# Three results of VectorE stay in PSUM banks: GLA's cumulative decay, the head norm's reciprocal root, and the SSD group's masked C.B

## The chip, the cores and the metric

The kernel runs on one core of one Trainium2 chip. Five engines of that core share the work, each with its own instruction stream: TensorE (PE in the profile, its weight loads PEld), VectorE (DVE), ScalarE (ACT), GpSimd (POOL) and SyncE (SP), which issues the transfers. There are two on-chip memories: SBUF, where operands live, and PSUM, eight banks of 128 x 512 fp32, where TensorE leaves its sums. The metric is the device time of one launch in microseconds.

## The reference

A decoder trunk of two layers over 1024 tokens, model width 1024, inner width 2048, all in float32. Layer 0 mixes tokens by gated linear attention (GLA), layer 1 by a Mamba-2 SSD mixer. Cut to what matters:

```
h = rmsnorm(x); q, k, v, g, low = split(h @ w_in)
a = log_sigmoid(low @ w_gate_up + bias) / 16          # 4 heads of 128 keys
# GLA, per chunk and head; S is the state (128 keys x 512 values)
b = cumsum(a)                                          # cumulative decay
attn = sum_d q[i,d] * k[j,d] * exp(b[i,d] - b[j,d])    # j <= i
o = (q * exp(b)) @ S + attn @ v
S = exp(b_last) * S + (k * exp(b_last - b)).T @ v
x = x + (rmsnorm(o) * head_norm * silu(g)) @ w_out     # head norm: mean over 512 values

# SSD, per group (8 groups of 4 heads), a = cumsum(dt * A)
y = (C B^T * exp(a_i - a_j), j <= i) @ (x * dt) + exp(a) * (C @ H) + x * d_skip
H = exp(a_last) * H + B.T @ (x * dt * exp(a_last - a))
x = x + rmsnorm(y * silu(z)) @ w_out
out = rmsnorm(x)
```

## The kernel before

Everything is held feature-major: a tile is 128 features by 512 tokens, so 1024 tokens are two passes t = 0 and t = 1, in the order GLA(0), GLA(1), SSD(0), SSD(1).

**Weight work.** The large projections run in three products per tile, from operands split into a high and a low part: high x high, low x high, high x low (`mm3`, L223 to L225, and L469 to L471 for v). A *unit* is one weight block of 128 x 512: its raw block is loaded (`wraw`), ScalarE makes the high half (`wh`, L171), and in the first pass GpSimd makes the low half (`wl`, L176) and SyncE stores it to DRAM; in the second pass the low half is loaded from there, and GpSimd has none of that work. `run` goes through the units one by one. The PSUM banks of the weight work have the tag "pp" (four), those of the mixers "mb" (four). Whatever empties a bank (`evac`) comes one unit later: in GLA L419 for the gate, L444 for q, L478, L480 and L482 for v (L478 on ScalarE in the first pass; in the second L480 on VectorE and L482 on ScalarE by turns), and L515, which adds an output projection to the residual.

**Sides.** The token mixers are generators that `run` steps at a given rate between units (0.95 steps a unit for a GLA head, 1.1 for an SSD group). So a mixer's instructions stand between the weight work of the next head or group. This is only the program's order: the framework's scheduler, which simulates a time line, then sets the final order of every engine's stream from the dependences and from when it expects operands. A tag with n buffers gives an n-th later tile the same memory, so it has to wait for the last reader of the earlier one.

**GLA's mixer, one head (L525 to L746).** L540 multiplies the low-rank gate into bank z. ScalarE and VectorE make log-sigmoid from it, and L551 scans it into b, an SBUF tile (`m2`). From b come, each as a subtraction on VectorE, an exponential on ScalarE and a multiplication on VectorE:

- kd (L558 to L560), the keys for the state, transposed by TensorE at L626;
- qd (L563, L564), the queries for the state;
- d (L569 to L573), keys and queries half a chunk apart;
- keys and queries at distances s = 16, 4 and 1 (L579 to L581 and L597 to L601; the queries of s = 16 and 4 are the tiles `o`, those of s = 1 the two tiles `raw`).

The products (L655) multiply keys by queries into four mb banks at once, VectorE places the results by masks (L616, L620) and from there attention, state (L712) and output o follow. Then the head norm: squares are summed on GpSimd (L321), `rstd_steps` spreads the sum over partitions with two matmuls into an mb bank p (L292, L293), `rstd_of` and `newton` (L307 to L313) make the reciprocal root. Its result r is an SBUF tile `rstd`. L738 multiplies o by the norm's weight and r, L739 (GpSimd) by the gate, and L743 and L744 split the product y into its two parts for the output projection.

**The SSD mixer, one group.** L1005 multiplies B and C into bank `pcb`. L1017 masks that to the lower triangle, into the SBUF tile `cbm` (`m2`). Four decay matrices M, one per head (two at L1044, two at L1067), are multiplied by it on VectorE and go into TensorE as operands. L1053 and L1055 advance the state H, L1028 and L1035 make the inputs.

What decides the order around the change is thus the scheduler, and the number of banks: four mb banks that z, the transposes, the products, the norm's p and the SSD's `pcb` take by turns.

Of the kernel before, what the change touches and what calls it, by code (L numbers as in the profile page):

```python
# [13 lines left out]
AF = mybir.ActivationFunctionType  # L14
ALU = mybir.AluOpType

P = 128
# [36 lines left out]
def hybrid_kernel(ctx: ExitStack, tc: tile.TileContext, xT, w_in0, w_gk, w_up, w_out0,  # L54
# [28 lines left out]
    def c3(ap, w=P):  # L83
        return ap.rearrange("p (n w) -> p n w", w=w)
# [198 lines left out]

    def rstd_steps(ssum, n, box, var=None):

        hi, lo = tl("t", NTMP, dt=F32R)[:], tl("t", NTMP, dt=F32R)[:]
        A.copy(hi, ssum)
        V.tensor_tensor(lo, ssum, hi.bitcast(F32), op=ALU.subtract)  # L290
        p = ps("mb")
        PE.matmul(p[:], onr[:], hi, start=True, stop=False)  # L292
        PE.matmul(p[:], onr[:], lo, start=False, stop=True)  # L293
        yield
        yield from rstd_of(p, n, box, var)

    def rstd_of(p, n, box, var):
        v = tmp() if var is None else var
        V.tensor_scalar(v, p[:], 1.0 / n, EPS, op0=ALU.mult, op1=ALU.add)
        r = tl("rstd", 3)[:]  # L300
        l = tmp()
        act(l, v, AF.Ln)
        act(l, l, AF.Exp, scale=-0.5)
        newton(V, r, v, l)
        box.append(r)
        yield
# [102 lines left out]
    class Gla:  # L409
# [115 lines left out]
        def mixer(self, h):  # L525
# [23 lines left out]
            for c in range(NC):  # L549
                cs = slice(c * P, (c + 1) * P)  # L550
                V.tensor_tensor_scan(b[:, cs], m[:, cs], l[:, cs], 0.0, op0=ALU.add, op1=ALU.subtract)  # L551
            yield

# [3 lines left out]
            kd = tmp()  # L557
            V.tensor_tensor(c3(kd), bc[:, :, P - 1:P].to_broadcast([P, NC, P]), bc, op=ALU.subtract)  # L558
            act(kd, kd, AF.Exp, scale=1.0 / 16)
            V.tensor_tensor(kd, k, kd, op=ALU.mult)  # L560
            yield
            qd = tl("x", 4)[:]
            act(qd, b, AF.Exp, scale=1.0 / 16)  # L563
            V.tensor_tensor(qd, q, qd, op=ALU.mult)  # L564
# [3 lines left out]
            dv = c3(d)  # L568
            V.tensor_tensor(dv, bc, bc[:, :, 63:64].to_broadcast([P, NC, P]), op=ALU.subtract)  # L569
            act(dv[:, :, 0:64], dv[:, :, 0:64], AF.Exp, scale=-1.0 / 16)  # L570
# [4 lines left out]
            def keys(s):  # L575

                e = tmp()
                bv = c3(b, s)
                V.tensor_tensor(c3(e, s), bv[:, :, s - 1:s].to_broadcast([P, T // s, s]), bv, op=ALU.subtract)  # L579
                act(e, e, AF.Exp, scale=1.0 / 16)  # L580
                V.tensor_tensor(e, k, e, op=ALU.mult)  # L581
                return e

            def queries(s, e, c0=0, c1=NC):
# [5 lines left out]
                cs = slice(c0 * P, c1 * P)  # L590
                bv, qv = c3(b[:, cs], w), c3(q[:, cs], w)
                after = []
                for i in range(3):
                    f, l = (i + 1) * s, 4 * s
                    o = sum(4 * s - (m + 1) * s for m in range(i))
                    after.append((e[:, :, o:o + l - f], f))
                    V.tensor_tensor(after[-1][0], bv[:, :, f:l], bv[:, :, f - 1:f].to_broadcast([P, n, l - f]),  # L597
                                    op=ALU.subtract)
# [131 lines left out]
            box = []  # L730
            yield from rstd_steps(ss, 512, box)
            for g in self.g[h]:
# [16 lines left out]
    class Ssd:  # L749
# [151 lines left out]
        def mixer(self, g):  # L901
# [110 lines left out]
            for c in range(NC):  # L1012
                for i in range(2):
                    o = (c % 2) * 256 + i * P
                    PE.transpose(px[c // 2][:, o:o + P], X[i][:, c * P:(c + 1) * P], ident[:])
            cbm = tl("m2", 1)[:]
            V.tensor_tensor(c3(cbm), c3(pcb[:]), trim[:].unsqueeze(1).to_broadcast([P, NC, P]), op=ALU.mult)  # L1017
            bh, bl = tl("ktok", 1, dt=F32R)[:], tl("t", NTMP, dt=F32R)[:]
# [383 lines left out]
```

## Time and profile before

| | |
|---|---|
| three runs | 1627.66, 1629.36, 1630.39 us; median 1629.36 |
| profiled execution | 1634.13 us, span 1632.4 us, mean granted clock of TensorE 0.992 |
| span by stage (from the trace) | first 69 us: norm, q, k and v of the first head; 69 to 421: GLA heads of t = 0; 421 to 770: GLA heads of t = 1; then SSD |

In the page's lines of groups a row reads: line, engine, operation, output <- inputs by the program's names, shape and type of both, how many; then, behind the bar, busy time in us and the mean ns of one; behind the second bar the idle time of the engine just before, and what ended most of it. In the lists of waits a row says which engine waited, at which tile and line, for which engine, tile and line, and then the us in all, the number of waits, and the longest one. A timeline row begins with the start in us from the span's start and the duration in us of that many instructions (x4). A row of a table by windows has the window's bounds, its length, the busy us and number of instructions of PE, PEld, DVE, ACT and POOL, the granted clock, the busy share of the DMA engines and what they moved in GB/s.

### The profile page before, as it was taken

What the parts mean: (1) busy time and instruction counts of PE and PEld (TensorE: products, weight loads), DVE (VectorE), ACT (ScalarE), POOL (GpSimd) and SP (SyncE); (2) the same over time, 40 slices, a digit from 0 to 9 for tenths busy, and PEclk for the clock granted to TensorE, in tenths of its full rate; (3) what the DMA queues carried; (4) which work ended last, traced back from release to release, by engine and by line L of the source; (5) the groups of instructions that cost most, each with busy time, mean ns of one, the idle gap of its engine ahead of it and who ended that gap; (6) DMA issues with size and microseconds to landing.
All of it is one profiled execution on the core that took longest, in us unless ns stands there. A gap on an engine that the chain in (4) does not pass through costs nothing.

```text
span 1632.4 us, 23995 instructions
## 1 busy us (share of the span) xinstructions
PE 1580.0 (97%) x8272; PEld 1308.2 (80%) x8272; DVE 984.5 (60%) x1579; ACT 947.2 (58%) x1788; POOL 692.8 (42%) x542
## 2 busy tenths in 40 slices
PE   7998999999999999999999999999999999999996
PEld 5777887877887888878888888887878888888886
DVE  6457567495736436295855534467885973355657
ACT  4435364543726355464874766665757777667843
POOL 6457566563412121126545655665523232222322
PEclk9999999999999999999999999999999999999999
DMA  7634556364585556463587555566666776656762
GB/s 232 185 123 131 176 174 201 123 201 146 191 269 193 162 166 217 154 207 120 176 262 228 175 188 173 173 209 216 208 193 186 257 235 221 204 177 189 260 197 84
DMA packets 172746, 309.30 MB, mean 189 GB/s; under 512 B 19088, under 2 KB 25104, under 8 KB 172624
## 3 DMA queue, kind: packets, MB, share of 16 engines
q1 hardware_dynamic: 172624, 307.77, 59.2%
q8 instruction: 65, 1.06, 0.3%
q14 instruction: 57, 0.47, 0.1%
HBM read 232.06 MB, written 75.63 MB: 188 GB/s over the span
## 4 chain that ended last, share of the span: by engine, by line
PE 78%; DVE 11%; ACT 4%; DMA 3%; issue 2%; POOL 2%; SPq 0%; DVEq 0%; ACTq 0%; POOLq 0%
PE pp L223 19%; PE pp L225 19%; PE pp L224 19%; PE pp L469 3%; PE pp L470 3%; PE pp L471 3%; PE mb L953 2%; PE mb L706 2%; DMA wraw<-w_in 2%; PE mb L705 2%; PE mb L946 1%; PE mb L655 1%; POOL wl L176 1%; PE mb L224 1%; PE mb L223 1%
## 5 line engine op out<-in xcount | busy, mean ns | idle before, releaser
L171 ACT CAST wh<-wraw 128x512 fp32r<-128x512 f32 x472 | 289.3, 618 | 379.3 <-PE pp L224 154.2
L223 PE MATMUL pp<-hh,wh 128*128 128x512 f32 x1184 | 468.3, 396 | 13.2 <-ACT wh L171 7.5
L176 POOL TENSOR_TENSOR wl<-wraw,wh 128x512 fp32r<-128x512 f32 x240 | 352.6, 1478 | 268.6 <-ACT wh L171 233.7
L224 PE MATMUL pp<-hl,wh 128*128 128x512 f32 x1184 | 464.1, 392 | 1.6 <-DVE hl L371 1.3
L225 PE MATMUL pp<-hh,wl 128*128 128x512 f32 x1184 | 463.2, 392 | 0.0
L223 PEld LDWEIGHTS pp<-hh,wh 128*128 128x128 f32 x1184 | 222.8, 188 | 65.3 <-ACT wh L171 9.0
L224 PEld LDWEIGHTS pp<-hl,wh 128*128 128x128 f32 x1184 | 222.9, 188 | 49.2 <-DVE hl L371 3.2
L225 PEld LDWEIGHTS pp<-hh,wl 128*128 128x128 f32 x1184 | 222.8, 188 | 46.5 <-issue 0.3
L223 PE MATMUL pp<-yh,wh 128*128 128x512 f32 x448 | 180.5, 403 | 5.2 <-DVE sg L419 2.4
L225 PE MATMUL pp<-yh,wl 128*128 128x512 f32 x448 | 178.5, 399 | 4.6 <-POOL wl L176 4.6
L224 PE MATMUL pp<-yl,wh 128*128 128x512 f32 x448 | 177.3, 396 | 0.0
L321 POOL TENSOR_TENSOR ss<-ss,t 128x512 f32<-128x512 f32 x53 | 74.4, 1403 | 81.7 <-ACT t L320 70.4
L223 PEld LDWEIGHTS pp<-yh,wh 128*128 128x128 f32 x448 | 85.6, 191 | 26.2 <-issue 4.5
L225 PEld LDWEIGHTS pp<-yh,wl 128*128 128x128 f32 x448 | 85.6, 191 | 24.4 <-POOL wl L176 5.1
L469 PE MATMUL pp<-wh,hh 128*128 128x512 f32 x256 | 100.8, 395 | 2.7 <-DVE m L444 2.7
L470 PE MATMUL pp<-wl,hh 128*128 128x512 f32 x256 | 101.0, 394 | 0.0
L471 PE MATMUL pp<-wh,hl 128*128 128x512 f32 x256 | 100.3, 394 | 0.0
L224 PEld LDWEIGHTS pp<-yl,wh 128*128 128x128 f32 x448 | 85.4, 191 | 18.2
L824 DVE SCALAR_TENSOR_TENSOR m<-pp,pr,m 128x509 f32<-128x509 f32 (+2 forms) x96 | 70.3, 742 | 40.0 <-ACT m L821 38.9
L824 DVE SCALAR_TENSOR_TENSOR x<-pp,pr,x 128x509 f32<-128x509 f32 (+2 forms) x96 | 71.2, 743 | 33.3 <-ACT x L821 32.2
L645 POOL TENSOR_TENSOR t<-v,t 128x512 fp32r<-128x512 f32 x28 | 40.6, 1460 | 101.5 <-ACT t L644 65.7
L739 POOL TENSOR_TENSOR t<-t,sg 128x512 f32<-128x512 f32 x32 | 50.9, 1621 | 75.3 <-ACT sg L98 68.3
(284 smaller groups left out, 2654.0 us busy)
## 6 DMA issues: line engine op xcount, KB each, us to landing
wraw<-w_in SPq DMA_DIRECT2D x352, 256.0 KB, 3.5
low_in<-wl SPq DMA_DIRECT2D x176, 256.0 KB, 3.8
wl<-low_in SPq DMA_DIRECT2D x176, 256.0 KB, 3.4
wraw<-w_out SPq DMA_DIRECT2D x128, 256.0 KB, 3.6
low_out<-wl SPq DMA_DIRECT2D x64, 256.0 KB, 4.3
v<-a_cum SPq DMA_DIRECT2D x64, 256.0 KB, 3.8
wl<-low_out SPq DMA_DIRECT2D x56, 256.0 KB, 3.4
xn<-x SPq DMA_DIRECT2D x43, 256.0 KB, 3.8
```

What stands on the lines that cost most here:

```text
L171: A.copy(hi[:, 0:w], raws[n][:, 0:w])
L176: G.tensor_tensor(lo[:, 0:w], raws[n][:, 0:w], hi[:, 0:w].bitcast(F32), op=ALU.subtract)
L223: PE.matmul(o, lh, rh, start=first, stop=False)
L224: PE.matmul(o, lh, rl, start=False, stop=False)
L225: PE.matmul(o, ll, rh, start=False, stop=last)
L321: eng.tensor_tensor(ss, ss, sq, op=ALU.add)
L469: PE.matmul(o, rh[kb][:, cs], wh[:], start=(kb == 0), stop=False)
L470: PE.matmul(o, rh[kb][:, cs], wl[:], start=False, stop=False)
L471: PE.matmul(o, rl[kb][:, cs], wh[:], start=False, stop=(kb == KB - 1))
L645: G.tensor_tensor(vl, v[c], vh.bitcast(F32), op=ALU.subtract)
L739: G.tensor_tensor(u, u, self.g[h][vb], op=ALU.mult)
L824: V.scalar_tensor_tensor(dst[:, s:], o[:, 0:T - s], col(C_CW + j * 32 + si), dst[:, s:], op0=ALU.mult, op1=ALU.add)
```

## The change

Three results are written to, or left in, a PSUM bank, so that the VectorE instructions that read them take one operand from PSUM and one from SBUF instead of two from SBUF.

1. **b.** After the scan ScalarE copies b into bank z, which until then held the gate's product (`A.copy(z[:], b)`, L553). Every subtraction (kd, d, keys, queries) takes its full-size operand from z, and its broadcast column still from b in SBUF; the exponential for qd reads z. The bank is held until the last of them.
2. **The head norm.** With `stay=True` the last instruction of `newton` writes r over p, the bank of the norm's sums. The four multiplications by r (L738, now L741) read it there. The other norms keep their SBUF tile.
3. **Masked C.B.** L1017 masks `pcb` in place; the four multiplications read it there. The tile `m2` isn't taken in SSD for it any more.

```diff
-        yield from rstd_of(p, n, box, var)
+        yield from rstd_of(p, n, box, var, stay)
 ...
-    def rstd_of(p, n, box, var):
+    def rstd_of(p, n, box, var, stay=False):
         v = tmp() if var is None else var
         V.tensor_scalar(v, p[:], 1.0 / n, EPS, op0=ALU.mult, op1=ALU.add)
-        r = tl("rstd", 3)[:]
+        r = p[:] if stay else tl("rstd", 3)[:]
 ...
                 V.tensor_tensor_scan(b[:, cs], m[:, cs], l[:, cs], 0.0, op0=ALU.add, op1=ALU.subtract)
+
+            A.copy(z[:], b)
+            bz, zc = z[:], c3(z[:])
             yield
 ...
-            V.tensor_tensor(c3(kd), bc[:, :, P - 1:P].to_broadcast([P, NC, P]), bc, op=ALU.subtract)
+            V.tensor_tensor(c3(kd), bc[:, :, P - 1:P].to_broadcast([P, NC, P]), zc, op=ALU.subtract)
 ...
-            act(qd, b, AF.Exp, scale=1.0 / 16)
+            act(qd, bz, AF.Exp, scale=1.0 / 16)
 ...
-            V.tensor_tensor(dv, bc, bc[:, :, 63:64].to_broadcast([P, NC, P]), op=ALU.subtract)
+            V.tensor_tensor(dv, zc, bc[:, :, 63:64].to_broadcast([P, NC, P]), op=ALU.subtract)
 ...
-                V.tensor_tensor(c3(e, s), bv[:, :, s - 1:s].to_broadcast([P, T // s, s]), bv, op=ALU.subtract)
+                V.tensor_tensor(c3(e, s), bv[:, :, s - 1:s].to_broadcast([P, T // s, s]), c3(bz, s), op=ALU.subtract)
 ...
-                    V.tensor_tensor(after[-1][0], bv[:, :, f:l], bv[:, :, f - 1:f].to_broadcast([P, n, l - f]),
+                    V.tensor_tensor(after[-1][0], zv[:, :, f:l], bv[:, :, f - 1:f].to_broadcast([P, n, l - f]),
                                     op=ALU.subtract)
 ...
-            yield from rstd_steps(ss, 512, box)
+            yield from rstd_steps(ss, 512, box, stay=True)
 ...
-            cbm = tl("m2", 1)[:]
-            V.tensor_tensor(c3(cbm), c3(pcb[:]), trim[:].unsqueeze(1).to_broadcast([P, NC, P]), op=ALU.mult)
+            cbm = pcb[:]
+            V.tensor_tensor(c3(cbm), c3(cbm), trim[:].unsqueeze(1).to_broadcast([P, NC, P]), op=ALU.mult)
```

Lines behind L551 are three higher in the changed kernel: L558 is now L561, L560 is L563, L597 is L600, L601 is L604, L626 is L629, L655 is L658, L738 is L741. The scheduler orders GLA's mixers anew; in SSD it leaves almost everything in place. Three places, all in the first head of t = 0 (b is the tile m_134, z is mb_643, kd the tile t_681 and then t_682, d t_708 and t_709, the keys of s = 16 t_721 and t_722).

VectorE behind the scan, before:

```order
L551 SCALAR_TENSOR_TENSOR m_134_651<-t_645,t_646 128x128 x4
L597 TENSOR_TENSOR raw_790<-m_134_651 128x64x3
L597 TENSOR_TENSOR raw_790<-m_134_651 128x64x2
L597 TENSOR_TENSOR raw_790<-m_134_651 128x64
L558 TENSOR_TENSOR t_681<-m_134_651 128x512
L569 TENSOR_TENSOR t_708<-m_134_651 128x512
L579 TENSOR_TENSOR t_721<-m_134_651 128x512
L597 TENSOR_TENSOR o_148_719<-m_134_651 128x8x48
L597 TENSOR_TENSOR o_148_719<-m_134_651 128x8x32
L597 TENSOR_TENSOR o_148_719<-m_134_651 128x8x16
```

and after:

```order
L551 SCALAR_TENSOR_TENSOR m_134_651<-t_645,t_646 128x128 x4
L561 TENSOR_TENSOR t_682<-m_134_651,mb_643 128x512
L563 TENSOR_TENSOR t_682<-m_72_361,t_682 128x512
L419 TENSOR_TENSOR sg_830<-pp_741,rstd_261 128x512
L567 TENSOR_TENSOR x_706<-m_67_338,x_706 128x512
L572 TENSOR_TENSOR t_709<-mb_643,m_134_651 128x512
L582 TENSOR_TENSOR t_722<-m_134_651,mb_643 128x512
L600 TENSOR_TENSOR o_148_720<-mb_643,m_134_651 128x8x48
L600 TENSOR_TENSOR o_148_720<-mb_643,m_134_651 128x8x32
L600 TENSOR_TENSOR o_148_720<-mb_643,m_134_651 128x8x16
```

The subtractions for s = 1 (`raw`) went from the front to the end of the head's list, an evacuation of the weight work (L419) stands among them, and the multiplication of kd (L560, now L563) directly behind its subtraction.

ScalarE at the same place, before:

```order
L98 ACTIVATE t_646<-t_646,ones 128x512
L171 CAST wh_808<-wraw_691 128x512
L98 ACTIVATE decg_679<-m_134_651 128x4
L98 ACTIVATE x_705<-m_134_651 128x512
L98 ACTIVATE raw_790<-raw_790 128x64x6
L98 ACTIVATE t_681<-t_681 128x512
```

and after:

```order
L98 ACTIVATE t_646<-t_646,ones 128x512
L171 CAST wh_809<-wraw_692 128x512
L553 COPY mb_643<-m_134_651 128x512
L98 ACTIVATE decg_680<-m_134_651 128x4
L98 ACTIVATE t_682<-t_682 128x512
L98 ACTIVATE x_706<-mb_643 128x512
```

The copy stands ahead of the head's other work on ScalarE, and the exponential for kd is ahead of the one for qd.

TensorE at the products, before:

```order
L469 MATMUL pp_979<-wh_896,hh_11_145 128x512
L470 MATMUL pp_979<-wl_897,hh_11_145 128x512
L471 MATMUL pp_979<-wh_896,hl_12_146 128x512
L655 MATMUL mb_832<-raw_799,m_72_361 64x160 x4
L655 MATMUL mb_831<-raw_790,m_72_361 64x160 x4
L469 MATMUL pp_981<-wh_863,hh_4_130 128x512
```

and after:

```order
L469 MATMUL pp_983<-wh_864,hh_4_130 128x512
L470 MATMUL pp_983<-wl_865,hh_4_130 128x512
L471 MATMUL pp_983<-wh_864,hl_5_131 128x512
L658 MATMUL mb_833<-raw_800,m_72_361 64x160 x4
L658 MATMUL mb_832<-raw_791,m_72_361 64x160 x4
L658 MATMUL mb_834<-o_149_721,t_780 64x96 x8
L658 MATMUL mb_835<-o_148_720,t_722 64x96 x8
```

The products stand further back in the weight work. Counted in matmuls of 128 x 512 from the head's L540, the first product stood behind 86, 120, 132 and 132 of them in the four heads of t = 0 and now stands behind 110, 149, 147 and 144; the transposes of kd stood behind 67, 96, 92 and 84, and now behind 51, 88, 84 and 84.

More of the change, by code (lines that the diff above doesn't have):

```diff
@@ L281, in small_units, with rstd_steps @@
             units.append((None if hf else (src, None), KB * 32, f, None, prep))
-    def rstd_steps(ssum, n, box, var=None):
+    def rstd_steps(ssum, n, box, var=None, stay=False):
         hi, lo = tl("t", NTMP, dt=F32R)[:], tl("t", NTMP, dt=F32R)[:]
@@ L590, in queries @@
                 cs = slice(c0 * P, c1 * P)
-                bv, qv = c3(b[:, cs], w), c3(q[:, cs], w)
+                bv, zv, qv = c3(b[:, cs], w), c3(bz[:, cs], w), c3(q[:, cs], w)
                 after = []
```

## The prediction

> **What bounds the kernel now.** I read the page's busy times first, then who TensorE waited for, then the two engines behind those waits.
>
> ```profile
> PE 1580.0 (97%) x8272; PEld 1308.2 (80%) x8272; DVE 984.5 (60%) x1579; ACT 947.2 (58%) x1788; POOL 692.8 (42%) x542
> ```
>
> TensorE is busy for 97% of the span and the change removes no matmul, so only its idle time can be won. The waits of TensorE, asked for in three stretches: the GLA heads of the first 512 tokens (69 to 421 us), those of the second (421 to 770), and the SSD layer.
>
> ```profile
> PE pp L225 <- POOL wl L176: 4.6, 1, 4.6
> PE mb L655 <- DVE raw L601: 3.4, 1, 3.4
> PE mb L626 <- DVE t L560: 2.4, 2, 1.4
> PE pp L223 <- DVE sg L419: 2.4, 2, 2.0
> PE pp L223 <- DVE acc L515: 1.7, 2, 1.3
> PE mb L655 <- DVE t L581: 0.5, 1, 0.5
> PE mb L223 <- DVE a L620: 0.5, 1, 0.5
> ...
> PE pp L223 <- DVE v L480: 4.2, 3, 1.4
> ...
> PE mb L946 <- DVE Hw L1055: 1.4, 1, 1.4
> ```
>
> In the first stretch 15.5 us wait for VectorE, or for GpSimd behind it; in the second 4.2; in the SSD layer 1.4 of some 8. A long wait costs more than itself. Four windows, each just after a long wait of the first stretch (busy us and count of TensorE, its weight loads, VectorE, ScalarE and GpSimd, then the granted clock), and last an undisturbed one:
>
> ```profile
> 92.80:96.80 4.00, 3.76 (x21) 2.90 (x22) 3.87 (x8) 0.63 (x1) 1.68 (x3) 0.64 0.45 150
> 160.20:164.60 4.40, 4.39 (x10) 3.36 (x11) 4.40 (x6) 1.06 (x2) 3.61 (x3) 0.50 0.64 167
> 257.40:261.10 3.70, 3.42 (x8) 2.77 (x9) 3.60 (x8) 1.31 (x3) 0.85 (x1) 0.54 0.82 284
> 373.40:377.20 3.80, 3.66 (x9) 2.93 (x10) 3.66 (x10) 2.21 (x5) 1.49 (x2) 0.55 0.42 139
> 165.40:169.80 4.40, 4.40 (x21) 3.60 (x20) 4.40 (x8) 3.02 (x6) 2.99 (x3) 0.98 0.84 292
> ```
>
> After the 4.6 us wait the clock was 0.50, and 10 matmuls ran where 21 do. Window length times the missing share of the clock gives what each dip lost: 1.4, 2.2, 1.7 and 1.7, 7.0 us together. So the first stretch holds 22.5 us.
>
> Why VectorE is late stands in its groups by shape (busy us, mean ns of one, idle before).
>
> ```profile
> L515 DVE TENSOR_TENSOR acc<-pp,acc 128x512 f32<-128x512 f32 x64 | 43.5, 687 | 62.4 <-PE pp L225 62.4
> L738 DVE SCALAR_TENSOR_TENSOR t<-o,pr,rstd 128x512 f32<-128x512 f32 x32 | 38.5, 1264 | 0.3
> L1067 DVE TENSOR_TENSOR raw<-raw,m 128x512 f32<-128x512 f32 x32 | 29.5, 950 | 7.4 <-ACT raw L98 7.4
> L712 DVE SCALAR_TENSOR_TENSOR x<-x,decg,mb 128x512 f32<-128x512 f32 x24 | 17.7, 739 | 0.0
> L1017 DVE TENSOR_TENSOR m<-mb,trim 128x512 f32<-128x512 f32 x16 | 11.0, 688 | 62.0 <-PE mb L1005 62.0
> L558 DVE TENSOR_TENSOR t<-m 128x512 f32<-128x512 f32 x8 | 5.4, 680 | 0.0
> ```
>
> L515, L712 and L1017 read one operand from PSUM ("pp", "mb") and take 687, 739 and 688 ns. L738 and L1067, the same shape with both tensors in SBUF, take 1264 and 950 on average; L558, also both in SBUF, 680. So two SBUF operands cost nothing by themselves, and sometimes a lot. GpSimd shows the other side, beside VectorE in the same microseconds of the second head:
>
> ```profile
> 152.35 10.78 POOL L176 TENSOR_TENSOR wl<-wraw,wh 128x512 fp32r<-128x512 f32 x3 [2.29 <-PE pp L225]
> ...
> 151.45 0.74 DVE L597 TENSOR_TENSOR raw<-m 128x192 f32<-128x192 f32 x3
> 153.91 2.09 DVE L597 TENSOR_TENSOR o<-m 128x384 f32<-128x384 f32 x6
> ```
>
> Three weight splits take 10.78 us, while VectorE runs an unbroken row of instructions with two SBUF operands. The first of them is the low half that TensorE waits for (4.6 us above). Either engine, then, holds the other off. The rows of L515, L712 and L1017 say that an instruction with one PSUM operand does not take part.
>
> **The change part by part.** The copy of b into bank z adds eight ScalarE instructions. No row shows an SBUF to PSUM copy; the bounds are 0.62 us (L320, SBUF to SBUF) and 0.70 (L544, from PSUM):
>
> ```profile
> L320 ACT ACTIVATE t<-t 128x512 f32<-128x512 f32 x29 | 17.9, 618 | 0.0
> L544 ACT ACTIVATE t<-mb,pr 128x512 f32<-128x512 f32 x8 | 5.6, 696 | 1.4 <-PE mb L540 1.4
> ```
>
> I take 0.65, nearer the plain copy. It stands on the path from the scan to every subtraction of the head; a gain from it is excluded, since nothing leaves ScalarE for it. The changed VectorE instructions are 16 per head (L558, L569, two of L579, twelve of L597), four L738 per head, and 64 multiplications by the masked C.B (L1044, L1067): 224. Their base price goes from L558's 680 ns to L1017's 688, so 8 ns each and 1.8 us in all, spread over the program. [...] Writing the root (L313) and the masked product (L1017) to PSUM has no row; I price both as now, bounds -0.05 and +0.1 us each, and 24 of them matter little.
>
> What the collisions cost goes with this: L738 32 x (1264 - 739) = 16.8 us of VectorE, L1067 32 x (950 - 688) = 8.4. Only what TensorE waits for counts. **Second stretch, L738.** In the row of the sixth head:
>
> ```profile
> 509.07 4.81 DVE L738 SCALAR_TENSOR_TENSOR t<-o,pr,rstd 128x512 f32<-128x512 f32 x4
> 513.80 1.27 DVE L480 COPY v<-pp 128x512 f32<-128x512 f32 x2
> ...
> 514.63 0.47 PE L223 MATMUL pp<-hh,wh 128*128 128x512 f32 x1 [1.40 <-DVE v L480]
> ```
>
> L480 frees the bank that TensorE wants and stands behind the four L738. Without collisions these take 4 x 0.74 = 3.0 us, so L480 starts 1.8 us sooner and the 1.4 us wait is covered; three heads, **-4.2 us**. Their order did not move.
>
> **First stretch, the mixers.** Here the order moves. The decay factors with s = 1, which went first, now go last, and the products (L655, now L658) stand 24, 29, 15 and 12 large matmuls later, since they need four banks and z holds one until the last L597. What must be done by then, without collisions, shows in the fifth head, where GpSimd is idle; with them, in the first:
>
> ```profile
> 428.70 0.73 DVE L597 TENSOR_TENSOR raw<-m 128x192 f32<-128x192 f32 x3
> ...
> 439.05 0.81 DVE L601 TENSOR_TENSOR raw<-m,raw 128x192 f32<-128x192 f32 x3
> ...
> 84.24 4.79 DVE L601 TENSOR_TENSOR o<-m,o 128x384 f32<-128x384 f32 x6
> 88.96 4.02 DVE L601 TENSOR_TENSOR raw<-m,raw 128x192 f32<-128x192 f32 x3
> ```
>
> Clean, the list takes 439.86 - 428.70 = 11.2 us. In the first head it runs from the scan's end to 92.98. Where it starts, counted from the head's first matmul L540, for the first two heads:
>
> ```profile
> 69.30 0.39 PE L540 MATMUL mb<-stp,wup 128*128 128x512 f32 x1
> 72.24 2.10 DVE L551 TENSOR_TENSOR_SCAN m<-t,t 128x128 f32<-128x128 f32 x4 [0.45 <-ACT t L98]
> ...
> 135.57 0.39 PE L540 MATMUL mb<-stp,wup 128*128 128x512 f32 x1
> 148.92 2.02 DVE L551 TENSOR_TENSOR_SCAN m<-t,t 128x128 f32<-128x128 f32 x4
> ```
>
> The first head's list is 92.98 - 74.34 = 18.6 us with two evacuations of 0.6 us in it: 6.3 us of collisions. With L634 and the second L579 and L581 (1.8 us), three evacuations (1.8), the copy (0.65) and the pause for kd's exponential, whose user L560 now directly follows (0.7), the changed list takes 16.2 us clean. It starts 5.0 us after L540; 110 large matmuls at 0.233 us (below), with some 0.4 for the four transposes, are 26.0 us: 4.8 us are left for collisions. In the second head the list has 18 us of work with five more evacuations and a split of y, starts 15.4 us after L540 less 1.8 for a faster L738, and 149 matmuls are 35.1 us: 3.5 us are left. The third and fourth come out between 3 and 5 in the same way, so about 4 in the mean. The 0.233 us are two rows of the undisturbed window, 19 starts apart:
>
> ```profile
> 165.77 0.40 PE L224 MATMUL pp<-yl,wh 128*128 128x512 f32 x1
> ...
> 170.20 0.40 PE L225 MATMUL pp<-yh,wl 128*128 128x512 f32 x1
> ```
>
> Fewer collisions than 6.3 us are due: the subtractions no longer take part, and GpSimd gets its turn in them instead of coming with a backlog. At an estimated 3 us, half of 6.3, each head just fits. So I take back the starved weight split (4.6 + 2.2), the first head's products (3.4 + 1.4), and L560 and L419 with their dip (2.4 + 2.4 + 1.7), 18.1 us; L560's transposes stand 16 matmuls sooner in the first head and 8 or fewer in the others, but its VectorE part comes 10 or more instructions sooner. For one head that still misses its place, wait and dip, I give 4 back. The rest of the stretch (L515, L581, L620 and a dip, 4.4) comes from norm instructions L350 and L354, which keep two SBUF operands: half of it. **-16.3 us.**
>
> **SSD.** The multiplications lose collisions, and one stands upstream of L1055's 1.4 us; TensorE's order is nearly the same. The masked product holds its bank to the last L1067; the banks that follow are fed by instructions behind L1028 anyhow. **-1 us**, between 0 and -2.
>
> The sum is -4.2 - 16.3 - 1.0 = -21.5 us, against the profiled execution's 1634.1 us around its span of 1632.4. That execution lies 4.7 us above the median 1629.4 of the runs shown, so part of its waits may be its own; I keep 18 of the 21.5 and set them against the median: **1611 us**, own range 1602 to 1619.
>
> **The rivals.** *Collisions only move.* L601, L560, L744 and L321 still read SBUF twice, and a GpSimd instruction that got its turn during a subtraction holds up the next of them. For it: the 4.79 and 4.02 us above are L601's own, and L744 right behind L738 is no better:
>
> ```profile
> L744 DVE TENSOR_TENSOR yl<-t,yh 128x512 fp32r<-128x512 f32 x32 | 35.6, 1146 | 2.9 <-ACT yh L743 2.8
> ```
>
> If a mixer keeps its 6.3 us, each of four heads overruns its place by 2.3 us and adds a dip of 1.5. With the norm's 4.4 that is 19.6, against 22.5 + 4.2 + 1.0 = 27.7 now: -8, 1621 us. [...]
>
> *Slower: the products wait in every head.* z keeps the fourth bank, the copy and the pause lengthen the list, and TensorE stands at L658 with all weight work behind it. With 10 us of collisions per mixer each head overruns by 6 us and dips by 2: 32 us, with the norm's 4.4 less 27.7 now, +8.7, 1638 us. It decides from about 7.8 us of collisions on. Against it: GpSimd gets no more instructions than before, and 6.3 us were measured with all of the list taking part.
>
> *No change.* The waits are dealt anew by other late work, such as ScalarE's evacuations of v, or ScalarE's own read of bank z holds VectorE up as GpSimd did: 1628 us. Against it: the three L480 waits have a single cause, and it goes.
>
> **How the numbers follow.** Forecast 0.60, moved collisions 0.20, no change 0.12, slower 0.08. Below 0.2% (3.3 us) a measurement cannot tell a change: faster than 1626.1 are the first two and a little of the third, 0.82; the same 0.10; slower 0.08. The range runs from the full sum with a clean SSD and norm stretch, 1600, over the moved collisions to the edge of no change, 1626.
>
> **What would show it.** L738 near 740 ns and L1067 near 690; no weight split above 2.5 us; no wait for L480 in the second stretch; L744 and L601 still mixed. Wrong would be waits at L658 above 2 us in several heads, or L597 slower than now.

## The result, and the profile after

The changed kernel takes 1609.4 us (median of 6 runs, 1607.5 to 1614.4) where the kernel before takes 1629.3: a ratio of 0.988, interval 0.9865 to 0.989. The forecast was 1611 us. The full sum of -21.5 us, of which the forecast kept 18, was near the mark; two of the terms that make it were not, and their errors cancel. That is what the runs below take apart.

The page's line of busy times:

```profile
PE 1570.2 (98%) x8272; PEld 1305.0 (81%) x8272; DVE 951.4 (59%) x1579; ACT 951.4 (59%) x1796; POOL 655.3 (41%) x542
```

VectorE is busy for 33 us less, GpSimd for 37, and the span is 24.6 us shorter (1607.8). Where: the trace cut at the same three places of the program, the first L540 of each pass over GLA and the small matmul (L268) that opens each pass over SSD. Of each row the first numbers are the window and its length, then the busy times; the last but two is the granted clock. First the kernel before, then the changed one; the rows are GLA t = 0, GLA t = 1, SSD t = 0.

```profile
69.30:421.70 352.40, 336.40 (x1725) 275.73 (x1723) 237.36 (x387) 171.22 (x308) 204.99 (x139) 0.98 0.51 162
421.70:766.90 345.20, 340.40 (x1793) 284.55 (x1791) 184.01 (x366) 171.65 (x315) 84.55 (x61) 1.00 0.58 187
766.90:1186.10 419.20, 412.35 (x2142) 340.91 (x2142) 253.47 (x354) 285.01 (x564) 240.21 (x184) 1.00 0.63 199
```

```profile
69.20:408.50 339.30, 328.65 (x1724) 272.32 (x1724) 222.92 (x388) 173.47 (x312) 180.10 (x139) 0.99 0.52 168
408.50:748.60 340.10, 339.61 (x1797) 284.73 (x1796) 180.30 (x365) 173.59 (x319) 76.11 (x61) 1.00 0.58 190
748.60:1161.70 413.10, 411.20 (x2142) 340.44 (x2143) 239.90 (x354) 284.51 (x564) 236.68 (x184) 1.00 0.63 202
```

GLA t = 0 is 13.1 us shorter (forecast 16.3), GLA t = 1 is 5.1 (4.2), SSD t = 0 is 6.1 (1). The second pass over SSD takes 446 us in both.

The groups by shape that answer to those shown of before (busy us, mean ns of one, idle before):

```profile
L741 DVE SCALAR_TENSOR_TENSOR t<-o,pr,mb 128x512 f32<-128x512 f32 x32 | 21.8, 743 | 0.3
L1070 DVE TENSOR_TENSOR raw<-raw,mb 128x512 f32<-128x512 f32 x32 | 20.8, 680 | 5.3 <-ACT raw L98 5.3
L747 DVE TENSOR_TENSOR yl<-t,yh 128x512 fp32r<-128x512 f32 x32 | 33.3, 1071 | 7.8 <-ACT yh L746 7.4
L561 DVE TENSOR_TENSOR t<-m,mb 128x512 f32<-128x512 f32 x8 | 5.5, 687 | 4.7 <-ACT mb L553 4.7
L553 ACT COPY mb<-m 128x512 f32<-128x512 f32 x8 | 4.7, 591 | 8.3 <-DVE m L551 8.3
```

L738's successor L741 went from 1264 ns to 743, L1067's L1070 from 950 to 680; the subtraction L561 takes 687 where L558 took 680. At 128 x 512 an operand in PSUM costs 7 ns at most here. One small form pays more: the 128 x 192 subtractions for s = 1 take 398 ns from PSUM in GLA t = 1 of the changed kernel and 360 from SBUF in that of the kernel before (396 and 365 in the two kernels below that have no weight splits on GpSimd), where those of 128 x 128 take 340 and 343. Written to PSUM, the root's last instruction (L313) takes 700 ns (825 in SBUF before, the mean of all norms), the masked product (L1020) 696 (L1017: 688). The copy takes 0.59 us. L747, which still reads SBUF twice, is at 1071 (1146 before).

What TensorE waits for on VectorE in GLA t = 0 now, from the list of waits (us in all, count, longest):

```profile
PE pp L223 <- DVE acc L515: 5.4, 3, 2.3
PE mb L658 <- DVE raw L604: 4.2, 2, 3.0
```

The starved weight split, the transposes of kd and L419 are gone from the list; in GLA t = 1 nothing of VectorE is left in it. But L515 has grown from 1.7 us to 5.4, and the products still wait in two heads. Both come from one thing, seen in the second head on VectorE (the first row is from the first head, for comparison):

```profile
82.50 1.08 DVE L604 TENSOR_TENSOR o<-m,o 128x384 f32<-128x384 f32 x3
...
144.32 2.46 DVE L551 TENSOR_TENSOR_SCAN m<-t,t 128x128 f32<-128x128 f32 x4
...
155.13 1.18 DVE L584 TENSOR_TENSOR t<-m,t 128x512 f32<-128x512 f32 x1
156.24 3.48 DVE L604 TENSOR_TENSOR o<-m,o 128x384 f32<-128x384 f32 x3
159.64 0.68 DVE L515 TENSOR_TENSOR acc<-pp,acc 128x512 f32<-128x512 f32 x1
...
166.33 2.69 DVE L604 TENSOR_TENSOR o<-m,o 128x384 f32<-128x384 f32 x3
168.94 2.54 DVE L604 TENSOR_TENSOR raw<-m,raw 128x192 f32<-128x192 f32 x6
```

on GpSimd:

```profile
154.22 3.25 POOL L176 TENSOR_TENSOR wl<-wraw,wh 128x512 fp32r<-128x512 f32 x2 [3.02 <-ACT wh L171]
157.42 0.77 POOL L606 COPY raw<-m 128x256 f32<-128x256 f32 x1
158.12 2.73 POOL L648 TENSOR_TENSOR t<-v,t 128x512 fp32r<-128x512 f32 x2
```

and on TensorE:

```profile
160.46 0.47 PE L223 MATMUL pp<-yh,wh 128*128 128x512 f32 x1 [2.05 <-DVE acc L515]
...
171.63 0.63 PE L658 MATMUL mb<-raw,m 128*64 128x160 f32 x6 [2.96 <-DVE raw L604]
```

The multiplications (L584, L604) still read SBUF twice: three of L604 take 3.48 us beside GpSimd's work, in the first head 1.08. The evacuation L515 stands behind them in VectorE's queue and is 2.05 us late, and 11 us later the products are 2.96 us late.

### The profile page after: what moved, and what is told of

The parts are those of the page before. It is cut to its first block, busy times and chain, and to the rows that moved or that the text cites. A ratio compares the mean times of both kernels' runs of the same rounds, so it can differ in the third digit from the quotient of the medians.

```text
span 1607.8 us, 24028 instructions
## 1 busy us (share of the span) xinstructions
PE 1570.2 (98%) x8272; PEld 1305.0 (81%) x8272; DVE 951.4 (59%) x1579; ACT 951.4 (59%) x1796; POOL 655.3 (41%) x542
## 4 chain that ended last, share of the span: by engine, by line
PE 78%; DVE 11%; DMA 4%; ACT 4%; issue 1%; POOL 1%; SPq 0%; DVEq 0%; ACTq 0%; POOLq 0%
PE pp L223 18%; PE pp L224 18%; PE pp L225 18%; PE pp L469 3%; PE pp L470 3%; PE pp L471 3%; DMA wraw<-w_in 2%; PE mb L956 2%; PE mb L709 2%; PE mb L708 2%; PE mb L658 1%; PE mb L949 1%; DVE o L604 1%; PE mb L223 1%; PE mb L224 1%
## 5 line engine op out<-in xcount | busy, mean ns | idle before, releaser
L223 PE MATMUL pp<-hh,wh 128*128 128x512 f32 x1184 | 468.5, 397 | 8.8 <-ACT wh L171 7.4
L176 POOL TENSOR_TENSOR wl<-wraw,wh 128x512 fp32r<-128x512 f32 x240 | 328.3, 1375 | 277.1 <-ACT wh L171 232.3
L223 PEld LDWEIGHTS pp<-hh,wh 128*128 128x128 f32 x1184 | 222.8, 188 | 60.3 <-ACT wh L171 9.0
L223 PE MATMUL pp<-yh,wh 128*128 128x512 f32 x448 | 177.9, 397 | 6.1 <-DVE acc L515 5.4
L223 PEld LDWEIGHTS pp<-yh,wh 128*128 128x128 f32 x448 | 84.2, 188 | 26.1 <-issue 2.8
L1038 POOL TENSOR_TENSOR t<-t,o 128x512 fp32r<-128x512 f32 x32 | 41.8, 1310 | 91.6 <-ACT o L1036 87.0
```

The costliest lines, as they stand in the source:

```text
L176: G.tensor_tensor(lo[:, 0:w], raws[n][:, 0:w], hi[:, 0:w].bitcast(F32), op=ALU.subtract)
L223: PE.matmul(o, lh, rh, start=first, stop=False)
L1038: G.tensor_tensor(xel[-1], xe, hi.bitcast(F32), op=ALU.subtract)
```

## The experiments

Each kernel ran beside the kernel before on the same chip, and ratios are to that. The stage times are cut as above.

| kernel | median us | ratio (interval) | GLA t = 0 | GLA t = 1 | SSD t = 0 |
|---|---|---|---|---|---|
| before, two traces | 1629 to 1631 | 1 | 352.4, 352.3 | 345.3, 345.2 | 419.1, 415.0 |
| changed, two traces | 1609.4, 1611.6 | 0.988 (0.987 to 0.989), 0.987 (0.984 to 0.990) | 339.3, 343.9 | 340.0, 339.3 | 413.1, 411.3 |
| part 1 alone (b) | 1622.4 | 0.995 (0.993 to 0.997) | 346.3 | 345.2 | 414.7 |
| part 2 alone (root) | 1618.2 | 0.993 (0.990 to 0.996) | 346.4 | 339.3 | 417.1 |
| part 3 alone (C.B) | 1625.3 | 0.997 (0.995 to 0.998) | 349.8 | 346.9 | 412.5 |
| parts 2 and 3 | 1615.3 | 0.991 (0.989 to 0.992) | 349.0 | 339.3 | 412.6 |
| changed order, old operands | 1621.3 | 0.994 (0.992 to 0.996) | 352.2 | 341.0 | 411.7 |
| before without splits | 1594.8 | 0.978 (0.976 to 0.980) | 327.5 | 345.4 | 406.5 |
| changed without splits | 1588.7 | 0.974 (0.972 to 0.977) | 326.4 | 339.3 | 406.5 |
| changed, q and k in banks | 1601.7 | 0.982 (0.979 to 0.984) | 331.7 | 339.5 | 412.1 |
| the same, copies behind b | 1595.3 | 0.979 (0.977 to 0.980) | 326.5 | 339.4 | 413.3 |

**Each part alone.** The other two parts of the change are taken back.

```diff
 part 2 alone and part 3 alone:
-            A.copy(z[:], b)
-            bz, zc = z[:], c3(z[:])
+            bz, zc = b, c3(b)
 part 1 alone and part 3 alone:
-            yield from rstd_steps(ss, 512, box, stay=True)
+            yield from rstd_steps(ss, 512, box)
 part 1 alone and part 2 alone:
-            cbm = pcb[:]
-            V.tensor_tensor(c3(cbm), c3(cbm), ...)
+            cbm = tl("m2", 1)[:]
+            V.tensor_tensor(c3(cbm), c3(pcb[:]), ...)
```

> Part 1 alone: b is copied to bank z and the subtractions read it there; the norm's root and the masked C.B are SBUF tiles as before. If the parts add up as the trace of the changed kernel reads (GLA t = 0 shorter by 13.1 us, GLA t = 1 by 5.3, SSD by 6.0), this one has most of the first: L600 near 680 ns for the full-size ones, no weight split above 2.5 us, 1616 us (1612 to 1620), and the three L480 waits of 1.4 us in GLA t = 1 stay. If the parts only work together, under 5 us are gained: above 1624.

> Part 2 alone: the head norm's root stays in its bank. Theory: four L738 take 3.0 us in place of 4.8, the three waits for L480 go, -4.2 in GLA t = 1 and some 2 us in t = 0, where the next mixer's scan stands behind L738: 1623 us (1621 to 1626). Rival (the waits are dealt anew): 1628, with other evacuations late where L480 was.

> Part 3 alone: C.B is masked in its bank. By the prediction 1 us, 1628. By the trace of the changed kernel, whose SSD is 6.0 us shorter at nearly the same order, 1623 (1621 to 1625), nearly all of it in the first 512 tokens of SSD, where GpSimd is busy; nothing in GLA.

Part 1 gave 1622.4 us, a smaller gain than expected; part 2 1618.2, a larger one; part 3 1625.3, between its two forecasts. The first two lie outside their ranges. So 0.5%, 0.7% and 0.3%; the sum of 1.6% is more than the 1.2% that they bring together, so they may take part of the same time, though the intervals together are as wide as this difference. In stages it is clearer. The 6 us of GLA t = 1 are part 2's alone: without it the stage takes 345 to 347 us in every trace, with it 339 to 341. SSD t = 0 is part 3's: 412.4 us in the mean of the seven traces with it and GpSimd's splits, 416.5 in the four without it. In GLA t = 0 part 1 and part 2 bring 6 us each, by one trace each. Part 3 leaves the order of this stage as it was and its trace still shows 2.5 us less there, so that much is chance. The waits of part 1 alone show what b does and what it doesn't:

```profile
PE pp L223 <- DVE acc L515: 6.2, 3, 3.0
PE mb L658 <- DVE raw L604: 5.4, 2, 2.9
PE pp L223 <- DVE v L480: 4.2, 3, 1.4
```

No weight split is waited for, L480 waits as before, and L515 and the products wait as in the changed kernel.

**Order or collisions?** Part 1 also moves instructions. In this kernel the copy is made and bank z is held as long as in the changed one, and chained dependences hold VectorE's list in the changed order, but all subtractions save the last of a head read b from SBUF. Around the list the order isn't quite the same: in GLA t = 0 four evacuations of the weight work, three of them in the first head, stand 3 to 11 places later in VectorE's stream than in the changed kernel, and a few instructions of the other engines stand elsewhere.

```diff
+            bz, zc = b, c3(b)
 ...
+                    zv = c3(z[:, cs], w) if s == 1 and i == 2 and c0 else bv
+                    behind(V.tensor_tensor(after[-1][0], zv[:, :, f:l], ...))
```

> The changed kernel with its order of instructions and with the copy to bank z held as long, but all subtractions save the last of each head read b twice from SBUF. Theory (collisions): the subtractions collide again, and the products stand where they stood: GLA t = 0 gives back most of its 13.1 us, 1620 us (1616 to 1626), L600 and L582 at more than 1.2 us where GpSimd is busy and weight splits above 2.5 us again. Rival (the new order of the mixers is what gained): 1609 to 1612.

> Parts 2 and 3 together, without the copy of b. Beside the run with the changed order alone (1621 us) and the changed kernel (0.988 of the time before) it splits part 1 into its order and its collisions. Theory: the later place of the products and the copy cost some 5 us by themselves (the run with the order alone has -0.2 us in GLA t = 0 although part 2 alone has -6.0 there), and the subtractions without collisions bring 13: 1615 us (1612 to 1619), GLA t = 0 shorter by 6 to 8. Rival (the order costs nothing; parts 1 and 2 take away the same waits): 1620 to 1624.

They took 1621.3 and 1615.3 us, as the theory had them; but GLA t = 0 of parts 2 and 3 is 3 us shorter, not 6 to 8. From parts 2 and 3 (0.991) to the changed order with the old operands (0.994) the kernel gets slower by some 6 us: the price of the later products and of the copy, as long as the subtractions collide. From there to the changed kernel (0.988) it gains some 11: what the subtractions' operand is worth in this order. Part 1 is a net 5 us. Its price shows in the waits of the kernel with the order alone:

```profile
PE mb L667 <- DVE raw L611: 7.6, 3, 3.2
PE pp L223 <- DVE acc L515: 6.3, 3, 3.4
...
PE pp L469 <- DVE m L444: 2.1, 1, 2.1
```

The products (here L667) wait in three of the four heads of t = 0. The wait for L444 belongs to an evacuation that stands 11 places later than in the changed kernel; in the same head TensorE waits for the end of the list afterwards in any case. No weight split is waited for in this kernel, although its subtractions collide: the longest split of GLA t = 0 takes 2.64 us, where the kernel before has one of 7.81 and the changed one none above 1.79. In parts 2 and 3 without the copy the old waits stand instead, with the row of GpSimd behind the second of them:

```profile
PE mb L657 <- DVE raw L603: 4.1, 2, 3.4
PE pp L225 <- POOL wl L176: 3.4, 1, 3.4
```

```profile
149.68 10.78 POOL L176 TENSOR_TENSOR wl<-wraw,wh 128x512 fp32r<-128x512 f32 x3 [2.30 <-DMA wraw<-w_out]
```

**Without GpSimd's splits.** Except for the first ones (three instructions in the trace), all low halves of the weights are loaded and none is made on GpSimd, in the kernel before and in the changed one.

```diff
-            if key in lows:
-                dma(lo[:, 0:w].bitcast(F32), lows[key][:])
+            if lows:
+                dma(lo[:, 0:w].bitcast(F32), lows.get(key, next(iter(lows.values())))[:])
```

> The kernel before, without GpSimd's weight splits: the first low half is made and stored, every other one is loaded from that block, so all low halves are the first one's (a load takes the place of each store). Theory (VectorE is late in the first pass because its instructions with two SBUF operands collide with GpSimd's splits): L558 and L597 at their clean times, the 15.5 us of waits and 7 us of dips in GLA t = 0 go but for one or two, SSD t = 0 gains some 5: 1604 us (1598 to 1611). Rival (something else holds VectorE up, such as ScalarE's reads or the order): the waits for L601, L560 and L419 stay, above 1618.

> The changed kernel without GpSimd's weight splits, the low halves as in the run before it. If the change gains by nothing but collisions with GpSimd, there is little left for it to gain here: within 6 us of the kernel before without splits, 1600 us (1595 to 1606). If reading from PSUM is worth something by itself, or the new order is, it is faster than that kernel by 10 us or more.

They took 1594.8 and 1588.7 us, both below their ranges. For the kernel before the stages show where: 6 us went ahead of the first head's L540 (63 us in place of 69), which the theory hadn't counted, and GLA t = 0 lost 24.9 us, nearly all of its waits and dips. The SSD layer as a whole is some 6 us shorter, near the 5 expected; the column of SSD t = 0 makes it look like more, because 14 matmuls move from there into the second pass over SSD, which takes 451 us in place of 446.

The difference between the two kernels is 6 us, and the stages put it into GLA t = 1 (345.4 against 339.3); in GLA t = 0 and SSD t = 0 they differ by 1.1 and 0.0. With the splits, the same change brings 10.7 and 4.9 us there (means of two traces each). So in these two stages its gain needs the splits. More than that the difference can't show, since TensorE is busy there for 327.0 of 327.5 us and for all of 406.5 in the kernel before already, and hardly anything is left to gain. Where the splits are felt shows in a line of the list. The eight largest multiplications for s = 16 and 4 in GLA t = 0, first in the kernel before as it is, then without the splits:

```profile
L601 DVE TENSOR_TENSOR o<-m,o 128x384 f32<-128x384 f32 x8 | 9.3, 1159 | 0.0
...
L601 DVE TENSOR_TENSOR o<-m,o 128x384 f32<-128x384 f32 x8 | 4.6, 570 | 0.0
```

What is left of VectorE's waits in the kernel before without splits, and the group behind it:

```profile
PE pp L223 <- DVE v L480: 4.2, 3, 1.4
```

```profile
L738 DVE SCALAR_TENSOR_TENSOR t<-o,pr,rstd 128x512 f32<-128x512 f32 x32 | 38.5, 1263 | 0.3
L739 POOL TENSOR_TENSOR t<-t,sg 128x512 f32<-128x512 f32 x32 | 51.2, 1628 | 122.2 <-ACT sg L98 104.1 <-DVE t L738 18.1
```

L738 is as slow as ever with no split beside it. It collides with its own consumer, L739 on GpSimd, which runs beside the next L738 (in the kernel before four L739 from 509.99 to 516.27 us, four L738 from 509.07 to 513.88); with the root in its bank both get faster, L739 from 1628 to 1326 ns in the two kernels without splits. That is why this part pays in the second pass too: in the kernel before four L738 take 4.81 us each time at 509, 601 and 693 us, and GpSimd makes no split between 457 and 737.

**The rest of the list.** If L604 and L584 are late for colliding, their other operand can go to PSUM as well. The changed kernel, with q and k copied to two more banks in the first pass:

```diff
+            q0, k0 = q, k
+            if not t:
+                qz, kz = ps("mb"), ps("mb")
+                A.copy(kz[:], k)
+                A.copy(qz[:], q)
+                q, k = qz[:], kz[:]
```

> The changed kernel, and in the first pass q and k copied by ScalarE into two more banks, from which the multiplications of kd, qd, d, keys and queries read them; VectorE's order is the same. Theory: the rest of the mixer's list loses its collisions too (L604 at 549 ns for 384 columns in place of up to 1654), so the waits of 4.2 us at L658 and 5.4 us for L515 behind the list go with their dips: 1598 us (1593 to 1604). Rival (the list is late for its start or its pauses for ScalarE, or the held banks delay the products): 1608 to 1615.

It took 1601.7 us, within the range and 4 us above its middle. The line of L604 (here L610) now has both kinds in it, t = 1 from SBUF ("m") and t = 0 from PSUM ("mb"). The last row is the changed kernel's, t = 0 alone:

```profile
L610 DVE TENSOR_TENSOR o<-m,o 128x384 f32<-128x384 f32 x8 | 5.5, 687 | 0.0
...
L610 DVE TENSOR_TENSOR o<-mb,o 128x384 f32<-128x384 f32 x8 | 4.3, 543 | 0.0
...
L604 DVE TENSOR_TENSOR o<-m,o 128x384 f32<-128x384 f32 x8 | 10.4, 1296 | 0.0
```

The form from PSUM is at 543 ns beside the splits, where the same eight instructions take 1296 from SBUF. The waits at the products and for L515 are gone; a new one has come:

```profile
PE pp L223 <- ACT v L478: 4.1, 2, 2.8
```

ScalarE has the two copies ahead of L478, which empties v's banks, since q and k are ready long before b is. So the copies were tied behind the copy of b:

```diff
-                A.copy(kz[:], k)
-                A.copy(qz[:], q)
+                for i in (A.copy(kz[:], k), A.copy(qz[:], q)):
+                    tc.add_manual_dep(i.ins, cz.ins.name, ORDER, reason="copy")
```

> The changed kernel with q and k in banks, and ScalarE's two copies of them held behind the copy of b, so that they no longer stand ahead of L478, which empties the banks of v. Theory: the two waits for L478 (2.8 and 1.3 us in the run with q and k copied early) shrink to the 0.2 of the changed kernel: 1597 us (1594 to 1601). Rival (the copies now delay the exponential of kd and the whole list by 1.2 us): the waits at L658 come back, 1602 to 1606.

1595.3 us, a ratio of 0.979 (0.977 to 0.980): faster than both kernels of this case. GLA t = 0 in it, as one window:

```profile
69.40:395.90 326.50, 326.03 (x1724) 271.57 (x1724) 202.54 (x388) 177.35 (x321) 177.17 (x139) 1.00 0.56 175
```

TensorE is busy for 326.0 of 326.5 us at full clock, with 139 instructions on GpSimd as ever. The stage takes what it takes without splits (326.4): the collisions on the path of this stage are gone.

**How firm the stage times are.** Both kernels once more, unchanged.

> The kernel before, unchanged, for a second trace of it. Part 1 alone, whose SSD order is that of the kernel before, had its first 512 tokens of SSD 4.4 us shorter. Theory: part of the waits of the first trace there (L1033 1.4, L1055 1.4, L1035 0.9 us) are that execution's own, and the stage comes out 2 to 4 us shorter, 415 to 417 in place of 419.2 us; the waits in GLA (L176 4.6, L601 3.4, L480 3 x 1.4) are the program's and come again. Rival: the stage takes 419 again, and what part 1 does in GLA reaches into SSD.

> The changed kernel, unchanged, for a second trace of it: GLA of the first 512 tokens 339 us (within 1.5), of the second 340, the first 512 tokens of SSD 413 (within 2), with the same waits for L515 (5.4 us) and L604 (4.2).

The kernel before repeats GLA to 0.1 us and every wait in it, and takes 415.0 us for SSD t = 0 in place of 419.1: 4 us there belonged to the first execution. The changed kernel came out at 343.9 us in GLA t = 0, 4.6 more than the first time and outside what was expected. Its waits for VectorE are about the same (9.8 us for L515 and L604 in place of 9.6); the clock is not. Behind the waits at the products of the second and the fourth head:

```profile
169.90:173.90 4.00, 3.59 (x39) 3.62 (x41) 3.86 (x13) 0.23 (x1) 0.00 (x0) 0.60 0.67 230
...
351.30:355.30 4.00, 3.71 (x39) 3.74 (x41) 4.00 (x7) 1.14 (x2) 1.59 (x1) 0.57 0.81 294
```

With those at 159.0 (0.68) and 255.2 (0.61) that makes four dips, 1.3, 1.6, 1.6 and 1.7 us by the missing share of the clock, where the first trace has one of 1.6: 4.6 us. So where waits of 2 to 3 us are left in GLA t = 0, one trace can be off by some 5 us, and the mean of two puts this stage's gain at 10.7 us. The small differences of GLA t = 0 in the table bear no more than that; the comparisons by medians stand beside them.

## Why the prediction was right, and where it was not

**Collisions, and the PSUM operand as the way out.** Right, and now shown: nearly the same order with other operands (1621 against 1609 us), one line with and without the splits (1159 against 570 ns), and the same line in the same stage with both operands in SBUF and with one in PSUM (1296 against 543 ns). One wait went for another reason than the one given, the starved weight split; that comes below.

**Second stretch, L738.** Forecast -4.2 us, measured -5.6 (means of two traces). The three L480 waits went. What the term left out: each wait of 1.40 us put 1.79 us between the starts of L540 and L223, in place of 0.23, which makes 4.7 us; the rest isn't accounted for. In the changed kernel:

```profile
495.79 2.72 DVE L741 SCALAR_TENSOR_TENSOR t<-o,pr,mb 128x512 f32<-128x512 f32 x4
498.43 0.68 DVE L480 COPY v<-pp 128x512 f32<-128x512 f32 x1
...
499.55 0.39 PE L540 MATMUL mb<-stp,wup 128*128 128x512 f32 x1
499.78 0.39 PE L223 MATMUL pp<-hh,wh 128*128 128x512 f32 x1
```

Four L741 take 2.72 us (forecast 3.0), and L480 is done before TensorE asks.

**First stretch, the mixers.** Here a term failed: -16.3 forecast, -13.1 and -8.4 in two traces. The waits that were taken back did go, though four dips are there again in the second trace. The first head's sum came true nearly to the digit:

```profile
72.19 1.94 DVE L551 TENSOR_TENSOR_SCAN m<-t,t 128x128 f32<-128x128 f32 x4 [0.45 <-ACT t L98]
...
92.43 0.81 DVE L604 TENSOR_TENSOR raw<-m,raw 128x192 f32<-128x192 f32 x3
...
94.98 0.76 PE L658 MATMUL mb<-raw,m 128*64 128x160 f32 x8
```

From the scan's end at 74.1 to 93.2 are 19.1 us, 2.9 over the clean 16.2 where 3 were estimated, and the products come 1.7 us later. (The fifth head, from which the clean times came, had three splits beside the end of its list, 7.67 us from 435.84 on; its VectorE times were clean even so.) But "each head just fits" was carried over from there to heads in which it fails. In the second head the list runs from the scan's end at 146.8 to 171.5 (rows above): 24.7 us against 18 clean, some 6.7 us of collisions where there was room for 3.5.

An estimate from the rows says the same of the others. Adding up what each instruction of the list takes beyond the time that the fastest quarter of its kind stays within, the four heads have 7.2, 6.8, 6.6 and 6.8 us of collisions before and 3.0, 8.0, 6.3 and 6.8 in the changed kernel (0.1 to 0.2 with q and k in banks too). So the 3 us per head, on which the term rests, held in the first head alone.

In the second head the list also starts 16.6 us after L540 (at 130.15), not 13.6: L741 is faster, but two L747 right ahead of the scan take 2.89 us. TensorE waits 3.12 us for L515 and 2.96 for the products. The 4 us given back for one late head cover that and the fourth head's 1.28. Not covered is L515: "half" of 1.7 us was to stay, and 5.4 are there, since the evacuations stand between the multiplications that collide.

Of the lists' multiplications together (L560 to L601 in the old numbering) the groups by shape add up to 87.2 us before and 91.7 after, of the subtractions to 63.5 and 57.1. So VectorE's list has hardly become faster than before. The kernel with the order alone divides this: 95.7 and 67.8 us there. The new order made the list slower, and the operand made it faster again, its multiplications too. GpSimd's splits take 24 us less in all, but 21 of these came with the order, where the subtractions still read SBUF twice. The kernel before, the order alone, and the changed kernel:

```profile
L176 POOL TENSOR_TENSOR wl<-wraw,wh 128x512 fp32r<-128x512 f32 x240 | 352.6, 1478 | 268.6 <-ACT wh L171 233.7 <-PE pp L225 9.2 <-DMA wraw<-w_in 7.0
...
L176 POOL TENSOR_TENSOR wl<-wraw,wh 128x512 fp32r<-128x512 f32 x240 | 331.4, 1390 | 287.4 <-ACT wh L171 252.9 <-DMA wraw<-w_in 9.0 <-DMA wraw<-w_out 8.2
...
L176 POOL TENSOR_TENSOR wl<-wraw,wh 128x512 fp32r<-128x512 f32 x240 | 328.3, 1375 | 277.1 <-ACT wh L171 232.3 <-DMA wraw<-w_out 17.6 <-DMA wraw<-w_in 7.7
```

So the starved split, 6.8 of the 18.1 us taken back, went with the new order; the prediction had put its end down to the subtractions' operand. In the kernel before, the longest split starts at 152.35 us and ends at 160.16, right behind L419 at 158.96, the first instruction with a PSUM operand after 7.5 us of VectorE instructions with two from SBUF. In the new order evacuations and pauses stand inside the list; which of them frees GpSimd isn't separated here.

The rival of the moved collisions had the better size, 6.3 us and more, in three of the four heads; its mechanism isn't shown, since the multiplications rise with the order alone and fall when the subtractions stop colliding. A part of this stage's gain, moreover, was L738's (part 2 alone has 5.9 us there, parts 2 and 3 have 3.3), most of which the prediction had put down to the subtractions; the copy and the later products cost about 6 us with the operands of before, which its sum had at nothing as long as each head fits.

**SSD.** Forecast -1 us, measured some 4, the difference of the means with and without part 3. The mechanism was the one named, L1067 to 680 ns; the size was read off one wait for L1055 of 1.4 us, beside which a second one of 0.6 stood in the same list. All waits for L1055 in this stage are 1.1 to 2.0 us in the four traces with splits and without part 3, and 0.3 to 0.6 in the seven with both. The wait for ScalarE's L1033, 0.5 to 1.4 us in those four, is gone but for 0.2 in one of the seven. That makes some 2 of the 4 us; where the rest went isn't shown, and the two traces of the kernel before differ by as much among themselves in this stage.

**The slower rival** did not come. It was to decide from 7.8 us of collisions in every head; by the estimate above there were 3.0 to 8.0, and only the second head had more than that. The kernel with the order alone comes nearer to it, and is slower by 6 us than the same kernel without the move.

**The sum.** -4.2, -16.3 and -1 make -21.5. The means of the traces are -5.6, -10.7 and -4.9, together -21.2, and the median moved by 19.9 where the forecast had kept 18. The total came out right because an overestimate in the first stretch met underestimates in the two others, and that is luck. The experiments that split the parts would have shown a wrong division even so; the total alone could not.

## What to carry to other kernels

Where VectorE and GpSimd work at the same time, count the SBUF operands of VectorE's instructions. In these runs those with two of them and GpSimd's held each other off: the 384 columns of L604 took 1296 ns beside the splits, those of L601 570 without them, and three splits took 10.78 us where the median of one is 1.30. Those that read one operand from PSUM did not take part (543 ns for the 384 columns, 743 for L741), at 7 ns more for 128 x 512 and some 30 for 128 x 192. Look for the price on both engines: an unbroken row of such instructions showed up here as a starved GpSimd (those 10.78 us) with VectorE at its clean times (L558 at 0.68 us). Another order freed GpSimd as well (331.4 us of splits in place of 352.6), but VectorE paid for it (95.7 us of the lists' multiplications in place of 87.2). And take the whole row out, not a part of it: in the changed kernel the instructions that are left go on colliding (three L604 in 3.48 us), and an evacuation queued among them comes late (L515 by 2.05 us). A copy that makes room for this was cheap only where it stood behind the evacuations of its own engine: TensorE waited 4.1 us for L478 with the copies ahead of it, 0.5 with them behind, at 1601.7 and 1595.3 us.

## What had not been expected

**One instruction collides with its own consumer.** L738 and L739 work on neighbouring tiles, and with no split beside them L738 still takes 1263 ns and L739 1628.

**The clock does not dip behind every long wait.** The prediction took a dip for granted behind each. In the first trace of the changed kernel the windows behind the waits of 2.05, 2.96 and 2.3 us (granted clock the last but two):

```profile
160.20:164.20 4.00, 3.00 (x12) 2.18 (x12) 4.00 (x13) 2.30 (x4) 2.13 (x3) 1.00 0.39 131
171.40:175.40 4.00, 3.77 (x59) 3.62 (x60) 3.83 (x12) 1.29 (x3) 0.99 (x1) 1.00 0.61 218
254.60:258.60 4.00, 3.56 (x21) 2.62 (x23) 4.00 (x10) 1.66 (x3) 0.89 (x1) 0.59 0.56 197
```

Only the third has one. In the second trace of the same kernel all three waits have theirs (0.68, 0.60, 0.61), the middle one behind a shorter wait of 2.63 us. So in these two traces the length of the wait doesn't settle whether 2 to 3 us of it cost a dip of some 1.6 us more: the same three places have one dip in the first trace and three in the second. What settles it isn't shown. For a forecast it means that a dip is a chance and not a price: of the 13.1 us won in GLA t = 0 in the first trace 5.4 are dips that are gone (7.0 us before, 1.6 now), in the second only 0.8 of 8.5.
